# v's weights stored as four blocks, their casts earlier, and the first products of v in another order, in a hybrid encoder layer

## The chip, the cores and the metric

The kernel runs on one NeuronCore of a Trainium2 chip. TensorE (PE) multiplies, VectorE (DVE), ScalarE (ACT) and GpSimd (POOL) do the elementwise work, SyncE (SP) issues most of the DMAs. Each engine works through its own queue in order; semaphores order the engines among each other. The metric is the device time of one execution in microseconds, as the median of several runs: 666.32 us before the change (three runs, 666.21 to 666.91).

## The reference

One encoder layer over 1024 tokens of width 1024: an embedding LayerNorm, one input projection whose columns are split into eight parts, neighbourhood attention beside a gated linear recurrence, a merge, an output projection and a last LayerNorm. What the change touches is the LayerNorm at the entrance and the columns of `v`:

```python
h = layer_norm(x, emb_ln_g, emb_ln_b)
...
proj = x @ w_in
q, k, v, z_a, u, z_b, g_a, g_b = jnp.split(proj, offs, axis=-1)
attn = neighbourhood_attention(q.reshape(hs), k.reshape(hs), v.reshape(hs), rpb)
```

`v` is columns 1024 to 1535 of the projection: a product of the 1024 x 1024 normalised tokens with a 1024 x 512 matrix.

## The kernel before

**Tiles.** The tokens are eight tiles of 128 (tile 0 to 7), each 128 x 1024 in float32. The contracted width of 1024 is eight slices k of 128. A float32 product is made of three: each operand is split into a high part (a cast to float32r) and a low part (what the cast leaves), and high times high, low times high and high times low are summed in one PSUM bank. In the code `"h"` is high tokens with high weights, `"a"` low tokens with high weights, `"w"` high tokens with low weights. So v of one token tile is 24 products into one bank (`v_part`, L320).

**The start.** The LayerNorm's gain and bias come as 16 rows, are transposed and spread by TensorE over four PSUM banks `gps[z][c]` (z: gain or bias, c: which half of the width). ScalarE copies each into SBUF (`gb_copy`, L213) for GpSimd, which can't use PSUM. Tiles 0, 1 and 3 are normalised by VectorE straight out of those banks (`ln_v`, L240: two operations for each half, L243 and L246); tile 2 and the later ones by ScalarE (`ln_scale`, L248, one operation at L253) and then GpSimd, which multiplies by the gain and adds the bias (`ln_g`, L255, four operations). A normalised tile goes out to DRAM (`keep`) and through TensorE, which transposes it in two halves of four slices into a PSUM bank each (`turn`, L266). ScalarE casts the transposes to the high part (`turn_hi`, L279), VectorE makes the low part (`turn_lo`, helper at L128).

**v's weights.** `load_wv(c)` (L191) loads two slices k, 512 KB, into a half of a staging tile; four such loads, c = 0 to 3, are called blocks 0 to 3 here. `wv_hi(k)` (L194) casts one slice to its high part on ScalarE, `wv_lo(k)` (L197) makes its low part on GpSimd. `qk_prep` does both for 128 columns of q.

**What sets the order.** The program's order is written out by hand for each engine's queue; the framework adds the semaphore waits. The DMAs of SP go out in this order: tile 0 of x (two halves), blocks 0 and 1, tile 1, blocks 2 and 3, tile 2, the first of q's weights, tiles 3 and 4, a small table; then the store of tile 0, tile 5, the store of tile 1, the second of q's weights, which goes into the buffer of the first, and tile 6. `warm_up` (L200) issues small products of zeros that keep TensorE busy. `bank` (L88) hands out four PSUM banks in the order of `places` (L86).

Of the kernel before, what the change touches and what calls it, by code (L numbers as in the profile page):

```python
# [15 lines left out]
P = 128  # L16
S = 1024
D = 1024
NK = D // P
# [4 lines left out]
HALF = 512  # L24
# [7 lines left out]
WARM = 18, 4, 6  # L32
# [35 lines left out]
def encoder_kernel(ctx, tc, x, gb1, gb, w_qk, w_v, w_s, w_ba, w_bb, w_gate, smalls, bias, w_out, out):  # L68
    nc = tc.nc
    V, A, G, PE, SP = nc.vector, nc.scalar, nc.gpsimd, nc.tensor, nc.sync  # L70
# [12 lines left out]
    hb12 = pool("hb12", "right")  # L83

    turns = []
    places = itertools.chain((0, 1, 2, 3, 0, 1, 2, 0, 2, 3, 1), itertools.cycle((2, 3, 0, 1)))  # L86

    def bank(name):  # L88
        if turns:
            return banks[0].tile([P, HALF], F32, tag=next(turns[0]), bufs=2, name=name)  # L90
        if banks[0] is ps0:
            return ps0.tile([P, HALF], F32, tag=f"b{next(places)}", bufs=1, name=name)
        return banks[0].tile([P, HALF], F32, tag="bank", name=name)
# [62 lines left out]
    wvs = [hts[0].tile([P, 4, HALF], F32, tag="ht4" + c, name=f"wvs{c}") for c in "hl"]  # L156
# [12 lines left out]
    def qk_hi(m):  # L169
        qk_w[m] = pair(wpl, [P, NK, P], f"wqk{m}", tag="w", bufs=2)  # L170
        A.copy(qk_w[m][0][:], qk_s[m][:])

    def qk_lo(m):
        hi, lo = qk_w[m]
        lo_of(G, lo[:], qk_s.pop(m)[:], hi[:])

    def qk_prep(m):
        qk_hi(m)
        qk_lo(m)
# [9 lines left out]
            SP.dma_start(xs[i][:], x[i])  # L189

    def load_wv(c):  # L191
        SP.dma_start(wvs[c // 2][:, 2 * (c % 2):2 * (c % 2) + 2, :], w_v[:, 2 * c:2 * c + 2, :])

    def wv_hi(k):  # L194
        A.copy(wv[0][k][:], wvs[k // 4][:, k % 4, :])

    def wv_lo(k):  # L197
        lo_of(G, wv[1][k][:], wvs[k // 4][:, k % 4, :], wv[0][k][:])

    def warm_up(n):  # L200
        for _ in range(n):
            PE.matmul(clock[:, :P], zero[:], zero[:], start=True, stop=True)
# [10 lines left out]
    def gb_copy(z, c):  # L213
        A.copy(gb_t[z][c][:], gps[z][c][:])

    def ln_stats(i):
        st, mv, e = (ln.tile([P, n], F32, tag=f"ln{n}{c}", bufs=2, name=f"ln{i}{c}")
                     for n, c in ((12, "t"), (2, "m"), (4, "e")))
        sts[i] = st, mv, e[:, 3:4], e[:, 0:3]
        sd, ve = sts[i][2:]  # L220
        for c in range(2):
            V.bn_stats(st[:, 6 * c:6 * c + 6], xs[i][:, halves[c]])
        V.bn_aggr(mv[:], st[:].rearrange("p (c s) -> p c s", c=2))
        V.tensor_scalar(ve[:, 0:1], mv[:, 1:2], EPS, -0.5, ALU.add, ALU.mult)

    def ln_root(i):
        st, mv, sd, ve = sts[i]
        A.activation(sd, mv[:, 1:2], AF.Sqrt, bias=eps_t[:])

    def ln_sums(i):  # L230
        ln_stats(i)
        ln_root(i)

    def ln_rstd(i):
        st, mv, sd, ve = sts[i]
        V.reciprocal(sd, sd)
        V.tensor_scalar(ve[:, 1:2], sd, sd, ve[:, 0:1], ALU.mult, ALU.mult)
        V.tensor_scalar(sd, ve[:, 1:2], 1.5, sd, ALU.add, ALU.mult)

    def ln_v(i, c):  # L240

        z, (st, mv, sd, ve), sl = xs[i], sts[i], halves[c]
        V.scalar_tensor_tensor(z[:, sl], z[:, sl], mv[:, 0:1], gps[0][c][:], ALU.subtract, ALU.mult)  # L243
        if c == 0:
            ln_rstd(i)
        V.scalar_tensor_tensor(z[:, sl], z[:, sl], sd, gps[1][c][:], ALU.mult, ALU.add)  # L246

    def ln_scale(i):  # L248

        z, (st, mv, sd, ve) = xs[i], sts[i]  # L250
        ln_rstd(i)
        V.tensor_scalar(ve[:, 2:3], mv[:, 0:1], -1.0, sd, ALU.mult, ALU.mult)
        A.activation(z[:], z[:], AF.Identity, bias=ve[:, 2:3], scale=sd)  # L253
# [12 lines left out]
    def turn(i, kk):  # L266
        tp = tps[i, kk] = bank(f"tp{i}_{kk}")
        for k4 in range(4):
            k = 4 * kk + k4
            PE.transpose(tp[:, k4 * P:(k4 + 1) * P], xs[i][:, k * P:(k + 1) * P], ident[:])  # L270

    def ti(i):
        return slice((i % 4) * P, (i % 4 + 1) * P)

    def tp4(i, kk):
        return tps[i, kk][:].rearrange("p (k t) -> p k t", k=4)

    def turn_hi(i, kk):
        A.copy(blocks[kk][i // 4][0][:, :, ti(i)], tp4(i, kk))  # L279

    def turn_lo(i, kk):
        hi, lo = blocks[kk][i // 4]
        lo_of(V, lo[:, :, ti(i)], tp4(i, kk), hi[:, :, ti(i)])
# [36 lines left out]
    def v_part(i, kind, ks):  # L320

        if i not in vos:
            vos[i], vn[i] = bank(f"v{i}"), 0
        for k in ks:
            a = blocks[k // 4][i // 4][kind == "a"][:, k % 4, ti(i)]
            PE.matmul(vos[i][:], a, wv[kind == "w"][k][:], start=vn[i] == 0, stop=vn[i] == 23)  # L326
            vn[i] += 1
# [3 lines left out]
    def v_hi(i):  # L331
        vs = outs["v", i] = ln.tile([P, H, 2, DH], F32R, tag="vs", bufs=2, name=f"vs{i}")
        A.copy(vs[:, :, 0, :], vos[i][:].rearrange("p (h d) -> p h d", d=DH))
# [63 lines left out]
    K0, K1, KS, BOTH = range(4), range(4, 8), range(8), range(2)  # L397

    A.dma_start(gb_row[:], gb1.rearrange("o z (r f) -> (o z r) f", f=P))
    load_x(0)  # L400
    load_wv(0)
    load_wv(1)
    load_x(1)
    load_wv(2)
    load_wv(3)
    load_x(2)
# [10 lines left out]
        gb_spread(z, c)  # L417
    warm_up(WARM[2])
    ln_sums(0)
    ln_v(0, 0)  # L420
    turn(0, 0)
    warm_up(WARM[2])
    wv_hi(0)
    wv_hi(1)
    turn_hi(0, 0)
    ln_v(0, 1)
    keep(0)
    load_x(5)
    turn(0, 1)
    warm_up(WARM[2])  # L430
    wv_hi(2)
    wv_hi(3)
    turn_hi(0, 1)
    turn_lo(0, 0)
    gb_copy(0, 0)
    wv_hi(4)
    wv_hi(5)
    ln_sums(1)
    turn_lo(0, 1)
    wv_hi(6)  # L440
    wv_hi(7)
    gb_copy(1, 0)
    for k in KS:
        wv_lo(k)
    qk_prep(0)
    for k in K0:
        v_part(0, "h", (k,))
        v_part(0, "a", (k,))
    v_part(0, "w", (0, 1))
    v_part(0, "h", (4, 5))  # L450
    v_part(0, "w", (2, 3))
    v_part(0, "h", (6, 7))
    v_part(0, "a", K1)
    ln_v(1, 0)
    ln_v(1, 1)
    keep(1)
# [1 line left out]
    load_x(6)  # L458
    turn(1, 0)
    turn_hi(1, 0)  # L460
    v_part(0, "w", (4, 5))
    v_part(1, "h", K0)
    turn(1, 1)
    for z in BOTH:
        gb_copy(z, 1)
    turn_hi(1, 1)
    v_part(0, "w", (6, 7))
    ln_stats(2)
    turn_lo(1, 0)
    ln_root(2)  # L470
    v_hi(0)
    ln_scale(2)
    turn_lo(1, 1)
    ln_g(2)
# [567 lines left out]
    for slot in range(7 * N_PAIR + 4):  # L1042
        p, k = divmod(slot, 7)
# [184 lines left out]
    for unit in range(-NT, H * NT + PV_LAG):  # L1228
        h, c = divmod(unit, NT)
# [356 lines left out]
    for slot in range(16 + len(plan)):  # L1586
# [28 lines left out]
        a, b, p = plan[slot - 16]  # L1615
# [11 lines left out]
    p, x, w = 3, banksX[3], banksW[3]  # L1627
# [10 lines left out]
    for n, part in pieces[2:] + pieces[:2]:  # L1638
        z = zs[p, 1, n]
# [88 lines left out]
```

## Time and profile before

| | |
|---|---|
| median of 3 runs | 666.32 us (666.21 to 666.91) |
| the profiled execution | 666.44 us |
| its span, first to last instruction | 664.7 us |
| TensorE clock granted, mean | 0.995 |
| TensorE busy | 651.7 us, 98% |
| VectorE, ScalarE, GpSimd busy | 79%, 58%, 60% |
| DMA moved | 113.42 MB, mean 171 GB/s |

The span starts with the first instruction and ends with the last; the profiled execution took 1.7 us more than its span. All times below are counted from the start of the span. A busy share says little where a stage of some 30 us is changed in a span of 665: the prediction reads that stage from the chain of waits and from the timelines of the engines. In those, a row is a group of instructions of one line that follow each other, with the time of the first and the time that the group took. Ends of matmuls are modelled, and a group's time is from the first start to the last end.

### The profile page before, as it was taken

Reading aid. Unit: us, or ns where it says so; the run is one execution under the profiler, and the core shown is the slowest. Engines: PE = TensorE matmul, PEld = TensorE weight load, DVE = VectorE, ACT = ScalarE, POOL = GpSimd, SP = SyncE. Lnnn points to the kernel's source line nnn. Section 1 sums busy time; section 2 is a strip of 40 time slices with the busy share of each in tenths; the row PEclk is TensorE's granted clock in tenths of the full one; section 3 lists DMA queues with packets and bytes.
Section 4 is the critical chain, followed back from the end, with each engine's and each line's share of the span. In section 5 each row is a group of like instructions: output and inputs, shape, how many; then the busy total and the mean of one; then the engine's idle time right before and its main releaser. Section 6 shows DMA issues by size and latency. Waiting matters only on the chain.

```text
span 664.7 us, 9463 instructions
## 1 busy us (share of the span) xinstructions
PE 651.7 (98%) x3129; PEld 543.7 (82%) x3129; DVE 523.8 (79%) x858; ACT 388.0 (58%) x684; POOL 396.9 (60%) x315
## 2 busy tenths in 40 slices
PE   8999999999999999999999999999999999999994
PEld 6888888888888888888788888888888888888883
DVE  6978867986899599879987697277777876994776
ACT  5556433256786677777666834277777744673242
POOL 4898263334576476658556455013552549989867
PEclk9999999999999999999999999999999999999997
DMA  8746616133334232522361548898977288333023
GB/s 314 258 159 222 202 51 204 67 111 115 123 101 145 71 111 93 192 97 95 127 222 55 190 162 286 303 345 274 351 262 245 64 301 294 113 116 127 26 102 127
DMA packets 52193, 113.42 MB, mean 171 GB/s; under 512 B 5472, under 2 KB 9904, under 8 KB 50608
## 3 DMA queue, kind: packets, MB, share of 16 engines
q1 hardware_dynamic: 51680, 112.28, 49.0%
q8 instruction: 25, 0.41, 0.3%
q10 hardware_dynamic: 464, 0.53, 0.2%
q14 instruction: 24, 0.20, 0.1%
HBM read 77.11 MB, written 35.68 MB: 170 GB/s over the span
## 4 chain that ended last, share of the span: by engine, by line
PE 90%; DVE 5%; DMA 2%; issue 1%; SPq 1%; POOL 1%; ACT 0%; POOLq 0%; DVEq 0%; ACTq 0%
PE a L134 32%; PE mb L134 13%; PE s L134 12%; PE x L134 6%; PE v L326 6%; PE w L134 5%; PE acc L1147 4%; PE q L134 3%; PE s L1101 3%; PE pt L1123 3%; PE g L794 2%; DMA wqk_s<-in_w_qk_dram 2%; DVE ws_l L128 1%; PE tp L270 1%; DVE uc L752 1%
## 5 line engine op out<-in xcount | busy, mean ns | idle before, releaser
L134 PE MATMUL a<-ht_h,ws_h 128*128 128x512 f32 x136 | 53.1, 391 | 0.0
L134 PE MATMUL a<-ht_h,ws_l 128*128 128x512 f32 x136 | 53.0, 389 | 0.0
L134 PE MATMUL a<-b_h,wa_l 128*128 128x512 f32 x136 | 53.0, 389 | 0.0
L134 PE MATMUL a<-ht_l,ws_h 128*128 128x512 f32 x136 | 52.9, 389 | 0.0
L134 PE MATMUL a<-b_h,wa_h 128*128 128x512 f32 x136 | 52.9, 389 | 0.0
L134 PE MATMUL a<-b_l,wa_h 128*128 128x512 f32 x136 | 52.9, 389 | 0.0
L1111 DVE CUSTOM_DVE_ANT_0 sc<-s,bias 128x384 f32<-128x384 f32 (+1 forms) x64 | 33.4, 522 | 21.5 <-PE s L1101 14.1
L1131 ACT CAST pt_h<-pt 128x384 fp32r<-128x384 f32 x64 | 29.0, 453 | 25.2 <-PE pt L1123 17.1
L1116 ACT ACTIVATE p<-sc,summ 128x384 f32<-128x384 f32 (+1 forms) x64 | 37.8, 591 | 5.3 <-DVE summ L1111 5.1
L134 PE MATMUL mb<-ya,wb_h 128*128 128x512 f32 x128 | 39.6, 389 | 0.0
L902 POOL CAST wb_h<-wb 128x512 fp32r<-128x512 f32 x9 | 7.0, 781 | 47.1 <-DMA wb<-in_w_bb_dram 47.1
L128 DVE TENSOR_TENSOR pt_l<-pt,pt_h 128x384 fp32r<-128x384 f32 x64 | 33.2, 519 | 2.1 <-ACT pt_h L1131 1.6
L128 POOL TENSOR_TENSOR ht_l<-t,ht_h 128x512 fp32r<-128x512 f32 x16 | 22.0, 1408 | 19.9 <-ACT ht_h L312 19.9
L326 PE MATMUL v<-wv,b_h 128*128 128x512 f32 x128 | 33.2, 400 | 0.5 <-ACT b_h L279 0.5
L1101 PE MATMUL s<-ks,qs 128*128 128x384 f32 (+1 forms) x128 | 31.3, 326 | 0.0
L134 PEld LDWEIGHTS a<-ht_h,ws_h 128*128 128x128 f32 x136 | 25.5, 188 | 5.9 <-issue 0.4
L1123 PEld LDWEIGHTS pt<-ident,p 128*128 128x128 f32 x176 | 23.1, 140 | 8.5
L134 PEld LDWEIGHTS a<-b_h,wa_h 128*128 128x128 f32 x136 | 25.5, 188 | 5.4
L134 PEld LDWEIGHTS a<-ht_l,ws_h 128*128 128x128 f32 x136 | 25.5, 188 | 5.4
L134 PEld LDWEIGHTS a<-b_l,wa_h 128*128 128x128 f32 x136 | 25.5, 188 | 5.3
L134 PEld LDWEIGHTS a<-b_h,wa_l 128*128 128x128 f32 x136 | 25.5, 188 | 5.3
L134 PEld LDWEIGHTS a<-ht_h,ws_l 128*128 128x128 f32 x136 | 25.5, 188 | 5.2
(548 smaller groups left out, 2264.7 us busy)
## 6 DMA issues: line engine op xcount, KB each, us to landing
ks<-k_d SPq DMA_DIRECT2D x8, 1024.0 KB, 7.9
h_d<-x SPq DMA_DIRECT2D x8, 512.0 KB, 4.9
v_d<-vs SPq DMA_DIRECT2D x8, 512.0 KB, 3.6
q_d<-q SPq DMA_DIRECT2D x8, 512.0 KB, 3.1
ga_d<-ga SPq DMA_DIRECT2D x16, 256.0 KB, 2.3
gb_d<-gb SPq DMA_DIRECT2D x16, 256.0 KB, 2.4
k_d<-k SPq DMA_DIRECT2D x8, 512.0 KB, 3.3
qs<-q_d SPq DMA_DIRECT2D x8, 512.0 KB, 4.9
```

The costliest lines, as they stand in the source:

```text
L128: eng.tensor_tensor(lo, full, hi.bitcast(F32), ALU.subtract)
L134: PE.matmul(o, a, b, start=first and i == 0, stop=last and i == len(prods) - 1, skip_group_check=not (first and last))
L270: PE.transpose(tp[:, k4 * P:(k4 + 1) * P], xs[i][:, k * P:(k + 1) * P], ident[:])
L326: PE.matmul(vos[i][:], a, wv[kind == "w"][k][:], start=vn[i] == 0, stop=vn[i] == 23)
L794: PE.matmul(o[:, n, :], w[:, 2 * d + b, :], us[b][:, n * HALF:(n + 1) * HALF], start=z == 0, stop=z == 1)
L902: G.tensor_copy(hi[:], st[:])
L1101: PE.matmul(o[:, :P * len(near(t))], q[:, t * P:(t + 1) * P], k[:, z, keys], start=z == 0, stop=z == 1)
L1111: V.tensor_tensor_reduce(s[:, :w], o[:, :w], heads[h][2][:, b0:b0 + w], -1.0, 3.0e38, ALU.add, ALU.min, accum_out=sums[h][0][:, t:t + 1])
L1116: A.activation(probs[h % 2][t][:], scs.pop((h, t))[:, :w], AF.Exp, bias=sums[h][0][:, t:t + 1], scale=-1.0, accum_out=sums[h][1][:, t:t + 1])
L1123: PE.transpose(tp[:, n * P:(n + 1) * P], probs[h % 2][t][:, z * P:(z + 1) * P], ident[:])
L1131: A.copy(pt[0][:, span(b)], tps[h, b][:, :P * len(near(b))])
L1147: PE.matmul(acc[g][:, d:d + w], vvs[h // 2][:, b, h % 2, :], pt[:, a:a + w], start=b in (1, 6) and z == 0, stop=z == 1 and b == (4, 7)[g])
```

## The change

In DRAM, v's weights were one array `[128, 8, 512]` (partition, slice, column), so that a block took 4 KB out of each 16 KB row. They become `[4, 128, 2, 512]`: each block is 512 KB in one piece. Bytes and transfers stay the same.

In the hand-written order of the start:

- The high casts of slices 0 to 3 stand ahead of the normalisation of tile 0 and of the casts of its transposes. Before, slices 0 and 1 stood ahead of the first cast of transposes and 2 and 3 ahead of the second.
- The first product of v's tile 0 stands ahead of the second half of tile 0's transposes, and one group of six zero products is gone.
- The other products of tile 0 are ordered h 1 to 3, w 0 and 1, a 0 to 3, w 2 and 3, h 4 to 7, a 4 to 7, w 4, then tile 1's first transposes, w 5, and so on.
- `gb_copy(0, 0)` goes from behind the second cast of transposes to behind the casts of slices 6 and 7; `gb_copy(1, 0)` from there to behind tile 1's first cast of transposes; `gb_copy(0, 1)` and `gb_copy(1, 1)` from ahead of tile 1's second cast to behind the eviction of v's tile 0 (`v_hi(0)`), ahead of `ln_scale(2)`.
- `qk_prep(0)` goes from ahead of tile 1's first cast to behind it.
- In `places` two entries change places; v's bank of tile 0 is now asked for one call earlier.

```diff
-    places = itertools.chain((0, 1, 2, 3, 0, 1, 2, 0, 2, 3, 1), itertools.cycle((2, 3, 0, 1)))
+    places = itertools.chain((0, 1, 3, 2, 0, 1, 2, 0, 2, 3, 1), itertools.cycle((2, 3, 0, 1)))
...
-        SP.dma_start(wvs[c // 2][:, 2 * (c % 2):2 * (c % 2) + 2, :], w_v[:, 2 * c:2 * c + 2, :])
+        SP.dma_start(wvs[c // 2][:, 2 * (c % 2):2 * (c % 2) + 2, :], w_v[c])
...
     ln_sums(0)
+    for k in K0:
+        wv_hi(k)
     ln_v(0, 0)
     turn(0, 0)
+    turn_hi(0, 0)
     warm_up(WARM[2])
-    wv_hi(0)
-    wv_hi(1)
-    turn_hi(0, 0)
+    v_part(0, "h", (0,))
     ln_v(0, 1)
     keep(0)
     load_x(5)
     turn(0, 1)
-    warm_up(WARM[2])
-    wv_hi(2)
-    wv_hi(3)
     turn_hi(0, 1)
     turn_lo(0, 0)
-    gb_copy(0, 0)
     wv_hi(4)
     wv_hi(5)
     ln_sums(1)
     turn_lo(0, 1)
     wv_hi(6)
     wv_hi(7)
-    gb_copy(1, 0)
+    gb_copy(0, 0)
     for k in KS:
         wv_lo(k)
-    qk_prep(0)
-    for k in K0:
-        v_part(0, "h", (k,))
-        v_part(0, "a", (k,))
+    v_part(0, "h", (1, 2, 3))
     v_part(0, "w", (0, 1))
-    v_part(0, "h", (4, 5))
+    v_part(0, "a", K0)
     v_part(0, "w", (2, 3))
-    v_part(0, "h", (6, 7))
+    v_part(0, "h", K1)
     v_part(0, "a", K1)
+    v_part(0, "w", (4,))
     ln_v(1, 0)
     ln_v(1, 1)
     keep(1)
     qk_load(1)
     load_x(6)
     turn(1, 0)
     turn_hi(1, 0)
-    v_part(0, "w", (4, 5))
+    qk_prep(0)
+    gb_copy(1, 0)
+    v_part(0, "w", (5,))
     v_part(1, "h", K0)
     turn(1, 1)
-    for z in BOTH:
-        gb_copy(z, 1)
     turn_hi(1, 1)
     v_part(0, "w", (6, 7))
     ln_stats(2)
     turn_lo(1, 0)
     ln_root(2)
     v_hi(0)
+    for z in BOTH:
+        gb_copy(z, 1)
     ln_scale(2)
...
-        "w_v": w_in[:, 1024:1536].reshape(NK, P, HALF).transpose(1, 0, 2),
+        "w_v": w_in[:, 1024:1536].reshape(4, 2, P, HALF).transpose(0, 2, 1, 3),
```

## The prediction

> **What bounds the kernel now.** I read the page first, then the chain of waits in order of time, then the timelines of ScalarE (ACT), VectorE (DVE), TensorE (PE) and GpSimd (POOL) over the first 30 us, and a table of stages for the DMA rate.
>
> ```profile
> span 664.7 us, 9463 instructions
> ```
> ```profile
> PE 90%; DVE 5%; DMA 2%; issue 1%; SPq 1%; POOL 1%; ACT 0%; POOLq 0%; DVEq 0%; ACTq 0%
> ```
>
> The end is set by TensorE, so this change in the first 30 us is worth what it moves the time from which TensorE runs without a gap. The chain in order of time shows that point:
>
> ```profile
> 16.05 1.05 ACT wqk_h L171
> 17.11 0.49 ACT b_h L279
> ...
> 17.64 1.20 PE v L326 x4
> 18.84 0.44 PE tp L270 x4
> 19.28 5.03 PE v L326 x22
> 24.31 2.87 PE q L134 x24
> 27.18 1.75 PE tp L270 x16
> ```
>
> Until 17.6 the chain is on other engines; from 17.64, v's products of token tile 1, it is on TensorE. TensorE's last wait there is for the cast of tile 1's transposes, which stands behind the cast of q's weights in ScalarE's queue:
>
> ```profile
> 8.34 1.14 ACT L195 CAST wv<-wvsh 128x512 fp32r<-128x512 f32 x2 [2.83 <-DMA wvsh<-in_w_v_dram]
> 9.39 0.58 ACT L279 CAST b_h<-tp 128x512 fp32r<-128x512 f32 x1
> 9.87 1.14 ACT L195 CAST wv<-wvsh 128x512 fp32r<-128x512 f32 x2
> 10.91 0.58 ACT L279 CAST b_h<-tp 128x512 fp32r<-128x512 f32 x1
> 11.39 0.59 ACT L214 COPY gb<-gps 128x512 f32<-128x512 f32 x1
> 12.21 1.15 ACT L195 CAST wv<-wvsl 128x512 fp32r<-128x512 f32 x2 [0.23 <-DMA wvsl<-in_w_v_dram]
> 13.26 0.29 ACT L228 ACTIVATE ln1e<-ln1m,eps_t 128x1 f32<-128x1 f32 x1
> 13.48 1.14 ACT L195 CAST wv<-wvsl 128x512 fp32r<-128x512 f32 x2
> 14.53 0.58 ACT L214 COPY gb<-gps 128x512 f32<-128x512 f32 x1
> 16.05 1.05 ACT L171 CAST wqk_h<-wqk_s 128x1024 fp32r<-128x1024 f32 x1 [0.94 <-DMA wqk_s<-in_w_qk_dram]
> 17.01 0.58 ACT L279 CAST b_h<-tp 128x512 fp32r<-128x512 f32 x1
> ```
>
> This is ScalarE's whole queue between 8.3 and 17.5. From start to start a pair of weight casts takes 1.05 us (8.34 to 9.39), a cast of transposes 0.48 (9.39 to 9.87). Block 0 of v's weights lands at 8.3, block 2 at 12.2, and q's weights, three transfers further, at 16.05: in steady state a 512 KB transfer lands every (16.05 - 12.21) / 3 = 1.28 us. So block 1 lands at about 9.6.
>
> ```profile
> 13.17 0.74 DVE L243 SCALAR_TENSOR_TENSOR x<-x,ln1m,gps 128x512 f32<-128x512 f32 x1
> ...
> 15.14 0.75 DVE L246 SCALAR_TENSOR_TENSOR x<-x,ln1e,gps 128x512 f32<-128x512 f32 x1 [0.61 <-ACT gb L214]
> ```
>
> (Columns of these timelines: start and duration in us, engine, line, operation, tiles, count, and in brackets the idle time before it with what ended it.) The row at 15.14 matters most: VectorE, scaling tile 1, waited 0.61 us for ScalarE's copy of the same gain bank, although both only read it. So in this program a VectorE read of a bank stands behind a ScalarE read that the program has earlier.
>
> **The change, part by part.**
>
> *The layout of w_v.* No operation is added; only the landings can move.
>
> ```profile
> 3.47 1.47 DVE L222 BATCH_NORM_STATS2 ln0t<-x 128x6 f32<-128x512 f32 x2 [2.48 <-DMA x<-in_x_dram]
> ```
>
> Bounds: tile 0's second half lands at about 4.2 (its statistics, two of some 0.7 us, started at 3.47 and ended at 4.94), so at the steady rate block 0 lands at 4.2 + 1.28 = 5.5; if the layout does nothing, at 8.3. Rates now:
>
> ```profile
> 3.50:6.00 2.50, 2.38 (x14) 2.38 (x14) 2.35 (x6) 0.37 (x2) 0.00 (x0) 1.00 0.80 210
> ```
> ```profile
> 20.50:22.50 2.00, 2.00 (x10) 1.66 (x9) 1.93 (x6) 1.32 (x2) 0.98 (x2) 1.00 0.85 170
> ```
> ```profile
> 19.94 0.33 SPq L189 DMA_DIRECT2D x<-in_x_dram  x1
> ```
>
> In the table of stages block 0 moved at 210 GB/s (last column), and 0.80 in the column before says that the DMA engines even stood idle; 512 KB in 1.28 us is 410. Its rows lie 16 KB apart, and after the change they are contiguous like those of x, which follow at the steady rate. Against this stands the second row: tile 5 of x, contiguous, issued at 19.94 when the queue had run empty, started at 170. I take block 0 at 6.0, nearer to the contiguous transfers that share its queue than to tile 5; both ends stay in the range. The blocks are then at 6.0, 7.3, 9.8 and 11.1 (tile 1 of x goes between the second and third), and all that is behind them in SP's queue comes 2.3 earlier.
>
> The Trainium skill (DMA: Bandwidth & Descriptors, "Latency and other measured facts") gives full rate for rows 512 KiB apart and a loss from 2 MiB on, so 16 KiB should cost nothing; by that rule the blocks land as now, which is the first rival. The 210 GB/s speak against it, the 170 of a contiguous load for it.
>
> *Four casts ahead of tile 0.*
>
> ```profile
> 7.57 0.66 PE L270 MATMUL tp<-ident,x 128*128 128x128 f32 x4 [0.34 <-DVE x L246]
> 8.07 0.50 PE L202 MATMUL clock<-zero 128*128 128x128 bf16 x6
> 9.08 0.66 PE L270 MATMUL tp<-ident,x 128*128 128x128 f32 x4 [0.52 <-DVE x L246]
> ```
>
> Casts 0, 1 run from 6.0, casts 2, 3 from 7.3 to 8.35; tile 0's first transposes are ready at 7.57 + 0.66 = 8.23, so their cast starts at 8.35 instead of 9.39. The second transposes wait for VectorE's second half of x, which this doesn't touch, and are ready at 9.08 + 0.66 = 9.74; one v product now stands ahead of them on PE, at most 0.1. Their cast starts at 9.8 instead of 10.91. Then casts 4, 5 at 10.3 (12.21 now), the root of tile 1, casts 6, 7 at 11.5 (13.48 now), and the first gain copy at 12.55, done at 13.15.
>
> *Gain copies.* The first copy of 11.39 goes behind all casts, and VectorE's first op on tile 1 is behind it by the rule of the row at 15.14: it starts at 13.15, now 13.17. Casting 2 us earlier gains nothing here. The copy that held the second op goes behind q's cast, so 0.61 of idle falls away; I take 0.55, since the semaphores between VectorE's small ops remain. Tile 1's transposes, which need that second op, start at 15.99 - 0.55 = 15.44 and are ready at 16.1:
>
> ```profile
> 15.99 0.63 PE L270 MATMUL tp<-ident,x 128*128 128x128 f32 x4
> ```
>
> The Trainium skill (PSUM — Partial Sum Buffer, "PSUM bank collisions raise a hardware error") says that two engines may not touch one bank at once, two reads included, so they have to be ordered. The trace agrees (0.61 us), and it speaks against putting the copy there.
>
> *q's weight cast behind tile 1's cast.* That cast starts at 16.1 instead of 17.01: 0.9 earlier, and so do v's products of tile 1 at 17.64. q's cast then runs at 16.6 to 17.65 and POOL's residue of it to 20.1 (21.43 now); the cover is that q's first product is at 24.31, 0.9 earlier after the change.
>
> *Product order, six zero matmuls less, places.* All free: after cast 7 (done 12.6) at most six products of tile 0 are left, 5.03 / 22 = 0.23 each, so PE has run out of them at 14.0 and waits for tile 1's transposes at 15.44. Without that cover each product behind a late operand would cost its wait. The zero matmuls (0.50 us for six, as at 8.07) run while PE waits. Exchanging two entries of places only undoes the earlier allocation of v's bank.
>
> *The last two gain copies, 1.05 us, now stand ahead of tile 2's scaling.*
>
> ```profile
> 19.99 0.58 ACT L333 CAST vs<-v 128x512 fp32r<-128x512 f32 x1
> 21.13 1.25 ACT L253 ACTIVATE x<-x,ln2e 128x1024 f32<-128x1024 f32 x1 [0.56 <-DVE ln2e L252]
> ```
>
> Now v's eviction starts at 19.99 and the scaling at 21.13. After: eviction 19.1, copies 19.6 to 20.65, scaling at 20.65, only 0.48 earlier. POOL follows:
>
> ```profile
> 9.04 5.04 POOL L128 TENSOR_TENSOR wv<-wvsh,wv 128x512 fp32r<-128x512 f32 x4 [7.74 <-ACT wv L195]
> 14.02 5.06 POOL L128 TENSOR_TENSOR wv<-wvsl,wv 128x512 fp32r<-128x512 f32 x4
> 19.02 2.41 POOL L128 TENSOR_TENSOR wqk_l<-wqk_s,wqk_h 128x1024 fp32r<-128x1024 f32 x1
> 22.45 5.30 POOL L259 TENSOR_TENSOR x<-x,gb 128x512 f32<-128x512 f32 x4 [1.02 <-ACT x L253]
> ```
>
> POOL's eight residues of v's weights follow ScalarE's casts and start 2.3 earlier too, so v's products with them are not late, and q's residue is done by 20.1 as above. The gains for tile 2 now end at 27.75, just when the third group of transposes (27.18 and two groups) wants them. They will end at 27.27, and TensorE, 0.9 ahead, waits 0.4 there. What is late next is thus tile 2's gain: 0.48 of the 0.9 is left.
>
> *q's next weights.*
>
> ```profile
> 26.96 1.05 ACT L171 CAST wqk_h<-wqk_s 128x1024 fp32r<-128x1024 f32 x1 [2.02 <-DMA wqk_s<-in_w_qk_dram]
> ```
>
> Their load on SP waits for POOL to free the buffer (21.43 now, 20.1 after), so ScalarE's 2.02 us wait before 26.96, which held tile 2's casts to 28.0 while its transposes began at 27.18, shrinks with it. What TensorE loses there no row shows alone; between 0 and the 0.8 from 27.18 to 28.0, most of it covered by the transposes' own 1.75, I take 0.1.
>
> **Sum:** -0.5 - 0.1 = -0.6. The profiled execution took 666.44 for its span of 664.7, so 665.84; the median shown, 666.32, is 0.12 lower: 665.7. With block 0 at 5.5 it is -0.7; past 6.0 every microsecond of block 0 costs about one, because ScalarE's queue shifts whole; the sign turns near 6.6.
>
> **Rivals.**
>
> *The layout does nothing (slower).* Block 1 lands at 9.6, and all of ScalarE's queue stands behind casts 2 and 3: tile 0's cast at 10.7 (9.39), the second at 12.2 because its transposes are now behind a product that waits for the first, casts 4, 5 at 12.7, 6, 7 at 14.0, the gain copy 15.0 to 15.6. VectorE starts tile 1 at 15.6 instead of 13.17, transposes at 17.9, products of tile 1 at 19.2 (+1.6), tile 2's scaling at 23.1 (+2.0). That less 0.1 gives 668.2. It decides from block 0 at about 7.9. For it: 170 GB/s of a contiguous load. Against: all other contiguous loads.
>
> *A slow start remains.* At tile 5's 170 GB/s for 2 us and the steady 410 for the other 180 KB, 512 KB take 2.45 instead of 1.28, block 0 lands at 5.5 + 1.2 = 6.7: 0.7 late against 6.0, so +0.1, 666.4, no change. For it speaks that row of tile 5, against it that the other contiguous loads of this queue came 1.28 apart. Its spread is 665.9 to 667.4.
>
> *The gain copy doesn't hold VectorE.* Then VectorE reaches tile 1 long before 13.15 and its transposes wait only for PE to run out of tile 0 at 14.0, 1.4 earlier than the forecast's 15.44: 664.3. Against it: the 0.61 us.
>
> *The early casts are eaten elsewhere*, for example by POOL's gains of tile 2, if the scaling stays at 21.13 because a copy waits for a bank's other reader: then its 27.75 stands, 666.3. Speaking for it is that POOL's end and TensorE's demand meet there already; against it, that those banks' other readers on VectorE are done by 17.3 (the op of 15.14 and two more halves of 0.75).
>
> **Chances.** Forecast 0.48, layout does nothing 0.16, slow start 0.26, copy doesn't hold 0.04, eaten 0.06. A measurement of this kernel tells 0.2% (1.3 us) from no change. Faster: the copy's rival and a small tail of the forecast, 0.07. Slower: the layout's rival and the end of the slow start, 0.18. Same: 0.75. The range 665.1 to 667.7 leaves out the first rival and the third; the forecast's own range is 665.4 to 666.1.
>
> **What would show it.** ScalarE's first weight cast near 6.0, four in a row before the first cast of transposes at 8.35; VectorE's first op on tile 1 idle behind a gain copy and starting near 13.15; products of tile 1 near 16.75; a wait of TensorE for POOL's x near 27. Wrong it is if the first weight cast still starts past 7.5, if VectorE doesn't wait for the gain copy, or if TensorE has no gap near 27.

## The result and the profile after

| | before | after |
|---|---|---|
| median of 5 runs each, same chip | 666.32 us (665.94 to 666.91) | 669.31 us (668.32 to 669.58) |
| the profiled execution | 666.44 us | 669.58 us |
| its span | 664.7 us | 667.8 us |
| ratio of the times | | 1.0042, 95% interval 1.0031 to 1.0053 |

The change made the kernel slower, by 3.0 us in the medians and by 3.14 us in the two profiled executions. The forecast was 665.7.

First ScalarE's queue after the change, from its timeline (columns as in the prediction):

```profile
7.74 2.42 ACT L195 CAST wv<-wvsh 128x512 fp32r<-128x512 f32 x4 [1.94 <-DMA wvsh<-in_w_v_dram]
10.07 0.58 ACT L279 CAST b_h<-tp 128x512 fp32r<-128x512 f32 x1
12.24 0.59 ACT L279 CAST b_h<-tp 128x512 fp32r<-128x512 f32 x1 [1.59 <-PE tp L270]
12.72 1.14 ACT L195 CAST wv<-wvsl 128x512 fp32r<-128x512 f32 x2
13.76 0.29 ACT L228 ACTIVATE ln1e<-ln1m,eps_t 128x1 f32<-128x1 f32 x1
13.95 1.14 ACT L195 CAST wv<-wvsl 128x512 fp32r<-128x512 f32 x2
14.98 0.58 ACT L214 COPY gb<-gps 128x512 f32<-128x512 f32 x1
18.54 0.58 ACT L279 CAST b_h<-tp 128x512 fp32r<-128x512 f32 x1 [2.97 <-PE tp L270]
...
22.93 1.27 ACT L253 ACTIVATE x<-x,ln2e 128x1024 f32<-128x1024 f32 x1
```

Block 0 let the first cast start at 7.74 (8.34 before), not at 6.0. Everything behind the four casts is late by that or more: tile 0's first cast at 10.07 (9.39 before, 8.35 forecast), its second at 12.24 (10.91 before, 9.8 forecast), the gain copy at 14.98 (12.55 forecast), tile 1's first cast at 18.54 (17.01 before). The next rows, from VectorE's and TensorE's timelines, show what the gain copy holds up:

```profile
15.60 0.75 DVE L243 SCALAR_TENSOR_TENSOR x<-x,ln1m,gps 128x512 f32<-128x512 f32 x1 [2.01 <-ACT gb L214]
```
```profile
19.18 1.18 PE L326 MATMUL v<-wv,b_h 128*128 128x512 f32 x4 [0.44 <-ACT b_h L279]
```

VectorE stood idle 2.01 us behind the copy and began tile 1 at 15.60 (13.17 before); v's products of tile 1 began at 19.18 (17.64 before).

The second loss is some 55 us further on, where nothing in the diff seems to reach. The chain of waits in order of time, before and then after:

```profile
73.68 10.88 PE q L134 x48
84.56 8.21 PE a L134 x36
92.76 2.72 PE s L134 x12
...
112.09 2.72 PE s L134 x12
```
```profile
75.34 10.89 PE q L134 x48
86.24 0.02 issue
86.26 0.61 ACT q L353
86.87 0.02 issue
86.89 0.70 DVE q L358
87.59 0.04 issue
87.64 8.45 PE a L134 x36
96.09 2.72 PE s L134 x12
...
115.13 2.72 PE s L134 x12
```

Before, `a` follows `q` at once. After, TensorE stops at 86.24 until ScalarE and VectorE have evicted the last sum of q (L353, L358). The page of after names this wait among its groups (columns: group, busy time and mean ns, idle time before it and what ended it); before has none there:

```profile
L134 PE MATMUL a<-b_h,wa_h 128*128 128x512 f32 x136 | 53.0, 390 | 1.4 <-DVE q L358 1.4
```

The third is the clock. The table of stages of after, in windows of 3.41 us (the last three columns are the granted clock, the DMA engines' share and GB/s):

```profile
7.48:10.89 3.41, 1.57 (x18) 1.31 (x17) 1.94 (x4) 2.76 (x5) 2.44 (x3) 1.00 1.02 413
10.89:14.30 3.41, 3.41 (x11) 2.77 (x11) 2.64 (x6) 2.06 (x5) 3.41 (x4) 0.50 1.04 410
14.30:17.71 3.41, 3.41 (x16) 2.55 (x14) 2.00 (x6) 1.27 (x3) 3.41 (x4) 1.00 0.95 362
```

From 10.89 to 14.30 the granted clock was 0.50: eleven matmuls in 3.41 us of a busy TensorE. In the window ahead of it TensorE had been busy for 1.57 us only, waiting for tile 0's late cast; before, the clock stays at full in this stage.

The balance of the two profiled executions is read where TensorE's weight loads for tile 2's v, for `a` and for later parts start, since from tile 2 on TensorE runs almost without a gap:

```profile
28.66 0.77 PEld L326 LDWEIGHTS v<-wv,b_h 128*128 128x128 f32 x4
...
84.17 0.19 PEld L134 LDWEIGHTS a<-b_h,wa_h 128*128 128x128 f32 x1
```
```profile
30.42 1.69 PEld L326 LDWEIGHTS v<-wv,b_h 128*128 128x128 f32 x8
...
87.64 0.19 PEld L134 LDWEIGHTS a<-b_h,wa_h 128*128 128x128 f32 x1 [1.84 <-DVE q L358]
```

Tile 2 starts 1.76 us late (30.42 - 28.66), `a` 3.47 us late (87.64 - 84.17): 1.71 more. In the chain, `s` is 3.33 late at 96.09 and 3.04 late at 115.13: about 0.4 comes back on the way, 0.29 of it in the `a` of 48 products ahead of that second `s`, which takes 11.17 in before and 10.88 in after. What is left, 3.0, with 0.1 of small differences further on, is the 3.14.

### The profile page after: what moved, and what is told of

The parts are those of the page before. It is cut to its first block, busy times and chain, and to the rows that moved or that the text cites. A ratio compares the mean times of both kernels' runs of the same rounds, so it can differ in the third digit from the quotient of the medians.

```text
span 667.8 us, 9451 instructions
## 1 busy us (share of the span) xinstructions
PE 652.7 (98%) x3123; PEld 545.5 (82%) x3123; DVE 522.4 (78%) x858; ACT 388.0 (58%) x684; POOL 395.5 (59%) x315
## 4 chain that ended last, share of the span: by engine, by line
PE 91%; DVE 5%; DMA 1%; issue 1%; ACT 1%; POOL 1%; POOLq 0%; SPq 0%; DVEq 0%; ACTq 0%
PE a L134 32%; PE mb L134 13%; PE s L134 12%; PE v L326 7%; PE x L134 6%; PE w L134 5%; PE acc L1144 4%; PE q L134 3%; PE s L1098 3%; PE pt L1120 3%; PE g L791 2%; PE tp L270 1%; DVE ws_l L128 1%; DMA wvsh<-in_w_v_dram 1%; DVE uc L749 1%
## 5 line engine op out<-in xcount | busy, mean ns | idle before, releaser
L326 PEld LDWEIGHTS v<-wv,b_h 128*128 128x128 f32 x128 | 24.3, 194 | 7.6 <-ACT b_h L279 2.8
L1120 PEld LDWEIGHTS pt<-ident,p 128*128 128x128 f32 x176 | 23.1, 140 | 8.5
```

Source lines behind the costliest of these rows:

```text
L1120: PE.transpose(tp[:, n * P:(n + 1) * P], probs[h % 2][t][:, z * P:(z + 1) * P], ident[:])
```

## The experiments

Two things are open here: whether the exchange in `places` makes the wait at 86.24, and which part of the order costs the 1.76 us at tile 2. The table has all runs; "first cast" is ScalarE's first cast of v's weights, which starts as block 0 lands, "tile 2" and "a" are the starts of TensorE's weight loads as above, from one profiled execution each. Each run was taken beside runs of before on the same chip (their median is 666.25 for the first four below `after`, 666.06 for the next four, 666.22 for the last three), and the ratio with its interval goes with these.

| run | first cast | tile 2 | a | median us | ratio to before, interval |
|---|---|---|---|---|---|
| before | 8.34 | 28.66 | 84.17 | | |
| after | 7.74 | 30.42 | 87.64 | 669.31 | 1.0042 (1.0031 to 1.0053) |
| bank put right | 7.57 | 29.69 | 85.10 | 667.58 | 1.0019 (1.0010 to 1.0027) |
| layout alone | 7.77 | 28.03 | 83.46 | 665.99 | 0.9997 (0.9988 to 1.0006) |
| order alone, bank put right | 8.14 | 30.27 | 85.67 | 668.55 | 1.0036 (1.0022 to 1.0050) |
| bank put right, more zero products | 8.11 | 30.27 | 85.65 | 668.08 | 1.0032 (1.0019 to 1.0044) |
| gain copy moved | 8.11 | 29.07 | 84.47 | 667.55 | 1.0023 (1.0014 to 1.0032) |
| copy moved and two casts back | 7.83 | 28.62 | 84.01 | 666.54 | 1.0007 (0.9998 to 1.0015) |
| rearranged on the order of before | 7.80 | 29.52 | 85.14 | 665.78 | 1.0003 (0.9994 to 1.0013) |
| weights read early once | 7.97 | 30.11 | 85.49 | 668.23 | 1.0037 (1.0025 to 1.0049) |
| rearranged, q's weights first | 8.07 | 27.91 | 83.33 | 665.36 | 0.9990 (0.9981 to 0.9999) |
| layout, q's weights first | 6.58 | 27.09 | 82.53 | 665.68 | 0.9993 (0.9984 to 1.0002) |
| layout, tile 1 loaded first | 9.00 | 29.18 | 84.60 | 666.96 | 1.0013 (1.0003 to 1.0023) |

**The bank put right.** `places` as before; the bank of tile 0's second transposes is asked for ahead of v's, although v's first product is issued first.

```diff
-    places = itertools.chain((0, 1, 3, 2, 0, 1, 2, 0, 2, 3, 1), itertools.cycle((2, 3, 0, 1)))
+    places = itertools.chain((0, 1, 2, 3, 0, 1, 2, 0, 2, 3, 1), itertools.cycle((2, 3, 0, 1)))
...
-        tp = tps[i, kk] = bank(f"tp{i}_{kk}")
+        if (i, kk) not in tps:
+            tps[i, kk] = bank(f"tp{i}_{kk}")
+        tp = tps[i, kk]
...
+    tps[0, 1] = bank("tp0_1")
     v_part(0, "h", (0,))
```

Expected:

> The changed kernel, but the bank of tile 0's second transposes is asked for ahead of v's bank, with the old order of places, so that the last product of q (q1_1) ends in bank 3 as before and not in bank 2, where the first product of the next stage begins. Theory (1.4 us of the loss of 3.0 is that product's wait for VectorE's eviction of q1_1 near 86 us): the wait is gone, 667.9. Rival (that wait only shows a lateness that the stage behind would take up anyway): 669.3 as changed.

The chain of this run at the same place, in order of time:

```profile
74.61 10.88 PE q L134 x48
85.49 8.24 PE a L134 x36
```

The wait is gone, `a` follows `q` at once, and from tile 2 to `a` it is 55.41 us (85.10 - 29.69) as in before (55.51), where after took 57.22. So the exchange cost 1.7 us. How it does so is read from the code, and no view here shows it: a named place gets its physical bank when it is first used, so exchanging two entries at the start exchanges two physical banks from there on, and the last sum of q then stands in the bank that the first sum of `a`, from another pool, uses next. The median falls by 1.7 us and stays 0.19% above before.

**The layout alone**, on the kernel before:

```diff
-        SP.dma_start(wvs[c // 2][:, 2 * (c % 2):2 * (c % 2) + 2, :], w_v[:, 2 * c:2 * c + 2, :])
+        SP.dma_start(wvs[c // 2][:, 2 * (c % 2):2 * (c % 2) + 2, :], w_v[c])
...
-        "w_v": w_in[:, 1024:1536].reshape(NK, P, HALF).transpose(1, 0, 2),
+        "w_v": w_in[:, 1024:1536].reshape(4, 2, P, HALF).transpose(0, 2, 1, 3),
```

> The kernel before with the layout of w_v alone. Theory (the layout brings block 0 some 0.6 us, and all loads behind it as much, q's weights at 15.4 instead of 16.05): first cast near 7.7, time 665.8 to 666.1. Rival (landings moved by chance between two executions, the layout does nothing): first cast at 8.3, 666.3. Rival (my forecast's landing at 6.0 holds when the casts' order is as before): first cast near 6.0.

The first cast starts at 7.77, 0.57 earlier in this execution, and tile 2 0.63 earlier. Both this and the median are as the theory has it, but the median can't be told from before's. The rate of the first transfers doesn't change with the layout either. This is the row of after for the stretch in which the prediction read 210 GB/s before; the blocks are contiguous now:

```profile
3.50:6.00 2.50, 2.35 (x14) 2.35 (x14) 2.01 (x5) 0.39 (x2) 0.00 (x0) 1.00 0.70 202
```

In the nine profiled executions with the new layout and the loads in the order of before (without the one with early reads) the first cast starts at 7.73 in the mean, eight of them between 7.57 and 8.11 and one at 6.58; in the two with the old layout at 8.34 and 8.14. So the layout may move block 0 by about half a microsecond, which is no more than block 0 scatters from one execution to the next; two executions of the old layout don't settle it.

**The order alone**, with the bank put right and the old layout:

```diff
-        SP.dma_start(wvs[c // 2][:, 2 * (c % 2):2 * (c % 2) + 2, :], w_v[c])
+        SP.dma_start(wvs[c // 2][:, 2 * (c % 2):2 * (c % 2) + 2, :], w_v[:, 2 * c:2 * c + 2, :])
```

> The changed kernel with the banks put right and w_v in its old layout: the order alone. Theory (each microsecond of block 0 costs one): 0.6 us slower than the kernel with the banks put right, 668.4 to 668.5, first cast near 8.3. Rival (the order costs nothing by itself): 666.3.

Against the run with the bank put right, the first cast is 0.57 later (8.14 - 7.57) and tile 2 0.58 later (30.27 - 29.69): one microsecond for each microsecond of block 0. The run with early reads further down, which is the same kernel but for one small transfer, lies on that line (7.97 and 30.11). At equal landings the new order is 1.86 us behind the old one: 29.89 at a first cast of 7.77, by that slope from 29.69 at 7.57, against 28.03 with the layout alone. The median, 668.55, is 0.97 above that of the bank put right, more than the landing explains; two of its five executions list a low clock, as told next.

**More zero products**: the six ahead of v's first product become 40, to keep TensorE busy until it can start.

```diff
     turn_hi(0, 0)
-    warm_up(WARM[2])
+    warm_up(40)
```

> The changed kernel with the banks put right and 40 instead of 6 zero products behind tile 0's first transposes, which fill TensorE's wait of 1.8 us. Theory (that wait took the granted clock to 0.5 for the 3.4 us from 10.9): clock 1.0 from 7.5 on, tile 0's second cast 0.5 earlier, 667.4. Rival (TensorE waits for other engines there, so its clock is free): 667.9 as with the banks alone.

The median, 668.08, is above what either theory says, and above the 667.58 without the 40: no gain in time is shown. The profiled execution, 669.11, lost some 1 us of that far from the change, at 434, where TensorE waits for work that stands behind a late load of `g`. The pair of profiles doesn't tell about the clock: with block 0 as in the order alone (8.11 and 8.14) tile 2 starts at the same 30.27, and neither execution has a window at half clock in the first stage. What tells is the mean clock that each execution lists. One window of 3.41 us at half clock lowers it by 0.0026 (3.41 x 0.5 / 665). The last microseconds of each profiled execution, when TensorE has run out of work, are at half clock too (in after from 662.84 on), so the twelve profiled executions without a window in the first stage list 0.994 to 0.997. A mean of 0.993 or less thus speaks for such a window; 0.994 can be either, and is what the profiled execution of after lists. In the five kernels whose TensorE waits for tile 0's late cast without those 40 (after, bank put right, order alone, gain copy moved, weights read early once), 14 of 36 executions list 0.993 or less. In all the others and in before it is 1 of 145, and none of the five with the 40 products. What such a window costs shows best in the run with the gain copy moved, which falls into two groups: five executions at 0.995 or 0.996 took 666.37 to 667.03, mean 666.65, and five at 0.992 or 0.993 took 668.08 to 668.35, mean 668.24. That is 1.6 us, about half of a window. In the profiled execution of after the window lay where TensorE had slack behind it: its tile 2 starts at 30.42, 0.56 later than the 29.86 that the run with the bank put right gives for a first cast at 7.74. The same 0.56 stands in ScalarE's wait for tile 0's second transposes, 1.59 in after and 1.03 with the bank put right.

**The gain copy moved** from behind the casts to beside the second copy, behind tile 1's first cast (on the bank put right, as the next one):

```diff
     wv_hi(7)
-    gb_copy(0, 0)
...
     qk_prep(0)
+    gb_copy(0, 0)
     gb_copy(1, 0)
```

> The changed kernel with v's bank back in its old place (as in the run with the banks put right, 667.58) and the first gain copy moved from behind the casts of v's weights to beside the second one, behind tile 1's first cast of transposes. Theory A (VectorE's first op on tile 1 is late only because it stands behind this copy): that op starts near 14.0 instead of 15.0 to 15.6 with no idle time behind a gain copy, the first product of tile 2 comes about 1.05 us earlier (28.6 with block 0 at 7.5, 29.2 with block 0 at 8.1), time 666.3 to 667.0. Rival B (the casts of v's weights, not the copy, hold tile 1: its root and transposes are late anyway): no gain over 0.2 us, 667.4 to 667.8.

VectorE's and ScalarE's timelines of this run:

```profile
13.88 0.74 DVE L243 SCALAR_TENSOR_TENSOR x<-x,ln1m,gps 128x512 f32<-128x512 f32 x1
```
```profile
17.07 0.58 ACT L281 CAST b_h<-tp 128x512 fp32r<-128x512 f32 x1 [2.17 <-PE tp L272]
```

VectorE's operation has no idle time ahead of it, tile 1's first cast starts at 17.07 (18.34 in the run with 40 zero products), and with block 0 at the same time as in the run with 40 zero products, tile 2 starts 1.20 earlier (30.27 - 29.07). Theory A held. The median misses its range because of the half-clock executions; the mean of the others, 666.65, lies in it.

**Copy moved and two casts back**: casts 2 and 3 again ahead of tile 0's second cast.

```diff
-    for k in K0:
-        wv_hi(k)
+    wv_hi(0)
+    wv_hi(1)
     ln_v(0, 0)
...
     turn(0, 1)
+    wv_hi(2)
+    wv_hi(3)
     turn_hi(0, 1)
```

> The same as the run with the moved gain copy, and besides casts 2 and 3 go back behind the second transposes of tile 0, where they stood before, so that ScalarE's queue no longer waits for block 1 ahead of tile 0's first cast. Theory A (each late operand ahead of tile 0's cast shifts the whole queue): another 0.2 us off where the copy is gone, 666.0 with block 0 at 7.5 and 666.6 at 8.1. Rival B (the casts' place costs nothing, the bank and the copy were all): the same as the run with the moved copy, within 0.1 us.

Tile 2 starts at 28.62, 0.17 earlier than the moved copy alone would with this block 0 (29.07 - 0.28). The larger gain is in the clock: none of its 11 executions lists less than 0.995, where five of ten did with the moved copy alone. TensorE's wait ahead of v's first product, which needs tile 0's first cast, shows what changed; first the run with the moved copy, then this one:

```profile
11.07 0.50 PE L328 MATMUL v<-wv,b_h 128*128 128x512 f32 x1 [2.54 <-ACT b_h L281]
```
```profile
9.51 0.50 PE L328 MATMUL v<-wv,b_h 128*128 128x512 f32 x1 [0.76 <-ACT b_h L281]
```

To the layout alone 0.53 is left at equal landings (28.62 against 28.03 + 0.06). GpSimd's timelines, here and then in the run with the layout alone, show where it sits:

```profile
22.47 2.66 POOL L259 TENSOR_TENSOR x<-x,gb 128x512 f32<-128x512 f32 x2 [1.58 <-ACT x L253]
```
```profile
21.85 2.66 POOL L259 TENSOR_TENSOR x<-x,gb 128x512 f32<-128x512 f32 x2 [1.01 <-ACT x L253]
```

GpSimd waits 0.57 longer for ScalarE's scaling of tile 2, which the two last gain copies now precede.

**Rearranged on the order of before**: what these readings point to, with the new layout and the banks of before.

```diff
     wv_hi(7)
-    gb_copy(1, 0)
+    gb_copy(0, 1)
+    gb_copy(1, 1)
...
-    qk_prep(0)
...
     turn_hi(1, 0)
+    qk_prep(0)
+    gb_copy(1, 0)
...
-    for z in BOTH:
-        gb_copy(z, 1)
     turn_hi(1, 1)
-    v_part(0, "w", (6, 7))
...
-    v_hi(0)
     ln_scale(2)
...
     v_part(1, "w", K0)
+    v_part(0, "w", (6, 7))
+    v_hi(0)
```

> The kernel before with the new layout, and the copies and casts that the readings point to: the gain copies of the second half of the columns right behind the casts of v's weights (ScalarE waits for q's weights there anyway), the copy that held VectorE's second op and the cast of q's weights behind tile 1's first cast, the scaling of tile 2 ahead of v's eviction, the last two residue products of tile 0 behind four of tile 1. Theory A (tile 1 is then held by nothing but the casts of v's weights, and tile 2's gains start as soon as GpSimd is free): first product of tile 2 near 27.3 with block 0 at 7.75 (28.03 in the run with the layout alone), time 665.2 to 665.6, ratio 0.998 to 0.999. Rival B (GpSimd's end or the load of q's next weights sets tile 2 anyway): no gain over the layout alone, 665.9 to 666.1.

The median, 665.78, lies between the ranges of the two theories. Nine executions took 665.3 to 666.0, three 667.5 to 668.0, the profiled one among them. SyncE's and then ScalarE's timeline of that one:

```profile
20.73 0.33 SPq L189 DMA_DIRECT2D x<-in_x_dram  x1
21.15 0.38 SPq L262 DMA_DIRECT2D h_d<-x  x1
21.63 0.37 SPq L167 DMA_DIRECT2D wqk_s<-in_w_qk_dram  x1
```
```profile
27.94 1.05 ACT L171 CAST wqk_h<-wqk_s 128x1024 fp32r<-128x1024 f32 x1 [3.99 <-DMA wqk_s<-in_w_qk_dram]
28.89 1.07 ACT L279 CAST b_h<-tp 128x512 fp32r<-128x512 f32 x2
```

q's next weights land at 27.9, behind tile 5 and the store of tile 1, and tile 2's casts stand behind their cast on ScalarE. Whether the other two long executions have the same cause, the next run tests.

**Rearranged, q's weights first**: that load goes ahead of both.

```diff
     keep(0)
-    load_x(5)
...
-    keep(1)
     qk_load(1)
+    load_x(5)
+    keep(1)
     load_x(6)
```

> The run with the rearranged copies and casts on the order of before (665.78; nine executions 665.3 to 666.0, three 667.5 to 668.0), and q's next weights loaded ahead of tile 5 and of the copy of tile 1 to DRAM, which stood ahead of them on SyncE. In its profiled execution (667.74) SyncE could start tile 5's load only at 20.73 (19.41 in the run with the layout alone), and q's next weights landed at 27.92 (26.20). Theory A (that chain of transfers makes the slow executions, and holds tile 2's casts in the others too): q's next weights are issued near 20.9 and land near 25, first product of tile 2 near 27.6, time 664.9 to 665.4, no execution above 666.5. Rival B (the transfer is slow by itself, whatever it is behind): landing near 26 to 28 again, 665.8 with some executions at 667.5 to 668.

```profile
21.18 0.33 SPq L167 DMA_DIRECT2D wqk_s<-in_w_qk_dram  x1
```
```profile
24.93 1.05 ACT L171 CAST wqk_h<-wqk_s 128x1024 fp32r<-128x1024 f32 x1 [0.74 <-DMA wqk_s<-in_w_qk_dram]
26.91 1.08 ACT L279 CAST b_h<-tp 128x512 fp32r<-128x512 f32 x2 [0.94 <-PE tp L270]
```

Theory A held: q's weights land near 25, tile 2's casts now wait for TensorE's transposes, not for weights, and the slowest of 11 executions took 665.77. The median, 665.36, is the lowest of all kernels here, 0.1% below before; the interval of the ratio ends at 0.9999, so the gain is only just told from none.

**Layout, q's weights first**: only this last move, on the layout alone.

> The kernel before with the new layout and q's next weights loaded ahead of tile 5 and of tile 1's copy to DRAM, nothing else. Theory A (in the order of before tile 2 is held by GpSimd's gains, which end near 27.1, as much as by q's weights): the cast of q's next weights at 25 instead of 26.23, first product of tile 2 at 27.8 instead of 28.03, time 665.6 to 666.0. Rival B (q's next weights alone hold it): first product near 27.0, 664.9 to 665.2.

The median, 665.68, lies in theory A's range, but its interval reaches past 1, so a gain is not shown. In its profiled execution block 0 happened to land 1.2 us earlier than in most and tile 2 started at 27.09, the earliest of all, but the execution took 666.03: TensorE gave about 1.1 of that back at 118.6, where it waits 0.80 for VectorE and the `a` behind takes 11.19 instead of 10.88. The chain:

```profile
115.90 2.73 PE s L134 x12
118.64 0.04 issue
118.67 0.70 DVE up L676
119.37 0.04 issue
119.42 11.19 PE a L134 x48
```

**Weights read early once, and tile 1 loaded first** ask why block 0 lands late whatever its layout. The first (on the bank put right) reads 64 bytes out of each 16 KB of v's weights on ScalarE's queue ahead of all loads; the second (on the layout alone) exchanges transfers:

```diff
+    A.dma_start(smh[:, 0:16], w_v.rearrange("c (a b) k n -> (c a) b (k n)", b=4)[:, 0, 0:16])
```
```diff
     load_x(0)
+    load_x(1)
     load_wv(0)
     load_wv(1)
-    load_x(1)
```

> The kernel with the banks put right, and one small transfer ahead on ScalarE's queue that reads 64 bytes out of each 16 KB of v's weights (they are not used). Theory A (block 0 is slow because its memory is read for the first time): block 0 lands near 6.0, all of v's first stage comes 1.5 us earlier and the first product of tile 2 is near 28.2, time 666.0; that would also be the landing that the prediction rests on. Rival B (the transfers of the first microseconds are slow whatever they read): block 0 at 7.5 to 8.1 as without it, time 667.4 to 667.8.

> The kernel before with the new layout, and tile 1 loaded ahead of the first two blocks of v's weights instead of behind them. Theory A (the third transfer on the queue is slow whatever it carries, since these are the first microseconds of the queue): tile 1 lands at 7.5 to 8.1, block 0 one steady transfer later at 8.8 to 9.4. Rival B (reading v's weights is slow at first): tile 1 lands near 6.0 and block 0 only after 8.0. The casts of v's weights come 1.3 us later in either case, so the time is near 667.2.

The early reads had landed at 4.94 (issued at 1.26, 3.7 to landing), and the first cast still started at 7.97: nothing gained, and rival B's landing. The median, 668.23, is above its range; three of the five executions list 0.992. With tile 1 in block 0's place, tile 1 landed at 7.62 and block 0 at 8.98, as theory A has it. So the third transfer on the queue lands at 7.5 to 8.3 in twelve of the thirteen profiled executions, whether it reads w_v in the old layout, w_v in the new one, or x. The thirteenth is the 6.58 of the layout with q's weights first, and what was different there the trace doesn't tell. Why the transfer is slow stays open.

## Why the prediction was wrong, point by point

**The layout's step failed.** "I take block 0 at 6.0" put the 210 GB/s of the first stage down to the rows of w_v. It belongs to the queue's first microseconds: contiguous blocks move at 202 GB/s there, and tile 1 of x, put in block 0's place, lands at 7.62. Tile 5's 170 GB/s on an idle queue had pointed that way. Block 0 came at 7.7, near the end of the range of bounds (5.5 to 8.3). By the measured slope that is 1.7 of the result, and without the half clock tile 2 would have started 1.2 late. The forecast's sum on its own premise stands: at one microsecond for each, 29.69 at a first cast of 7.57 gives tile 2 at 28.12 for 6.0, 0.54 ahead of the 28.66 of before, where the sum had -0.6. No run reached 6.0 in this order, so this is drawn out beyond the points that were measured. The page cited there (DMA: Bandwidth & Descriptors of the Trainium skill, "Latency and other measured facts"), by which the rows' distance costs nothing here, was the better guide: 0.9997 for the layout alone. Of the prediction's own signs of being wrong the first came, a first cast past 7.5. The second did not: VectorE waits for the gain copy. The third came too, in the main: all that TensorE waits at tile 2's transposes is 0.03, at 29.57.

**The first rival was nearly right**: its tile 1 on VectorE at 15.6, its products of tile 1 at 19.2 and its scaling of tile 2 at 23.1 are the 15.60, 19.18 and 22.93 of after. Part of that is luck: it put block 0 at 8.3, after had it at 7.74, and the 0.56 of the half clock, which the rival did not have, makes up the difference. Its chain is right all the same: in the order alone, with block 0 at 8.14 and no half clock, the three are 15.44, 19.01 and 22.78. Its 668.2 lacks the bank.

**"All free" failed twice.** "Exchanging two entries of places only undoes the earlier allocation of v's bank" was read from the start alone; the exchange costs 1.71 at `a`, of which 0.4 comes back. And of the product order and the zero products it was said that PE waits anyway. With tile 0's first cast late, v's first product waits for it, and the second transposes wait behind that product: ScalarE waits 1.03 for them with the bank put right, where the prediction had "at most 0.1". That wait also left TensorE busy for so little of a window that the clock was halved in some executions: 0.56 in the profiled one, 1.6 where it can't be hidden. No run moves that product alone; the 1.20 of the gain copy, the 0.17 of the two casts and the 0.53 at tile 2's gains come to 1.90, about the order's 1.86, without it.

**What held.** VectorE's read behind ScalarE's copy (2.01 us of idle; 1.20 of path when the copy is moved); the copies ahead of tile 2's scaling, which give back about 0.5; q's next weights as a small term that stands ahead of tile 2's casts. By the measured slope the sign turns with block 0 near 6.5 (28.66 for tile 2), where the prediction had 6.6; but the chance of that was sized by a landing of 6.0, and only one of thirteen profiled executions came near it.

**The sum as measured**, in the profiled executions: the order with block 0 at its real time +1.2, half clock +0.56, bank +1.71, what comes back behind `a` -0.4, the rest +0.1: 3.1.

## What to carry to other kernels

Where a pool hands out PSUM banks in a written order, exchanging two entries is a change to every later sum in that pool and to the next pool's first sums: look at the last evictions of the stage ahead of calling it free. Ahead of the first operand that may come late, put as little as possible on an in-order queue, and measure when that operand lands before building an order on it. A wait of TensorE can cost more than its own time, since here it halved the clock for the 3.41 us behind it in some executions; with two casts put back, which shortened the wait from 2.54 to 0.76, none of 11 executions shows it. Zero products in the wait left no low clock in five executions either, but no shorter time.

## What the runs showed of the hardware

- The half clock came in one whole window of 3.41 us, after a window in which TensorE was busy for 1.57 us of it, with its longest gap 1.84. At the end of the kernel it comes again; the row is of after, from 662.84 on:

```profile
662.84:667.79 4.95, 0.00 (x0) 0.00 (x0) 0.94 (x3) 0.00 (x0) 1.77 (x2) 0.50 0.59 212
```

  The stretch at full clock between the two, 648.54 us from 14.30 on, is 190 times 3.413. In the other twelve profiled executions the one stretch at full clock, from its start in the first 8 us to the half clock at the end, is 651.95 or 655.36, which is 191 or 192 times 3.413. (Ahead of that start the traces have no clock on record, and the column prints 1.00.) So the windows run in one grid, and the end of each trace tells where its windows lie. Laid out like this, the least busy window that was followed by full clock has 1.66 us of work in it. It is in the run with the gain copy moved:

```profile
6.87:10.28 3.41, 1.66 (x20) 1.44 (x18) 2.01 (x3) 2.02 (x4) 1.48 (x2) 1.00 1.01 394
10.28:13.69 3.41, 2.62 (x13) 2.21 (x14) 2.57 (x6) 2.39 (x6) 3.41 (x3) 1.00 1.03 419
```

  From that start on all windows with 1.66 or more of work were followed by full clock, and all with 1.57 or less, at the ends too, by 0.50. The bound of these thirteen traces thus lies between 1.57 and 1.66 of 3.41 us, a little under half. It also tells chance from cause: the order alone had only 0.99 of work between 7.48 and 10.89, but its windows begin at 6.38 and 9.79, share that wait between them with 2.04 and 2.11 of work, and the clock stayed.

  The Trainium skill (TensorE: Matmul & The Clock Gate, "What's actually happening") tells of a free-running window of 3413 ns, and half rate after an idle one. The length agrees, and that only some executions of one kernel are hit fits windows that run free of the kernel. That an idle window is needed does not agree: TensorE was at work for nearly half of this one.
- The first transfers on the queue are slow for their place, not for what they read: 7.5 to 8.3 for the landing of the third in twelve of thirteen executions, then about 1.28 us for each one behind.
